# A decoder block on one core: the early write into an 8 KB tile, done only up to the second RWKV group's keys

## The chip, the cores and the metric

The kernel runs on one core of a Trainium2 chip. A core has five engines with their own instruction streams: TensorE (PE; PEld is its weight load), VectorE (DVE), ScalarE (ACT), GpSimd (POOL) and SyncE (SP, which issues most of the transfers). They wait for each other by semaphores. The metric is the device time of one execution in microseconds. Before the change it was 1347.75 us, the median of three runs (1347.14 to 1352.83).

## The reference

One decoder block in float32, 256 positions of width 2048, with a memory of 256 rows of the same width. In short:

```python
p = rms_norm(h, norm_mix) @ w_in                      # one combined projection
y_rwkv = rwkv7_group(p[..., :RWKV_COLS], ...)         # 16 heads x 64
y_att  = dsa_group(p[..., RWKV_COLS:], positions)     # 8 heads x 128, 64 keys a query
h = h + concat([y_rwkv, y_att]) @ w_mix_out
h = h + memory_cross_attention(rms_norm(h, norm_cross), rms_norm(mem, norm_mem), w_q, w_kv, w_o)
u = rms_norm(h, norm_mlp) @ w_up                      # 2048 -> 8192
h = h + square(relu(u)) @ w_down
return rms_norm(h, norm_final)
```

The part around the change is the RWKV group. Its recurrence over positions

```python
sa = einsum('bhvk,bhk->bhv', state, -kk_t)
state = state * w_t + sa * (kk_t * a_t) + v_t * k_t
y_t = einsum('bhvk,bhk->bhv', state, r_t)
```

is worked out by chunks of 64 positions: products inside a chunk as matrices (Gram products), a triangular system, then the state from chunk to chunk. The 16 heads are done as two groups of eight. The other part it touches is the keys of the memory, `rms_norm(mem, norm_mem) @ w_k`.

## The kernel before

**Weights.** All weights stream from memory through four buffers of 512 KB (`raw`, L181) and are split into a high part `whi` (ACT, L187) and a low part `wlo` (DVE, L188), three buffers of each. A product of activations and weights is three matmuls: high by high, high by low, low by high (L215 to L217 with 256 columns, L227 to L229 with 512). The activations are split in the same way into `xhl`. The transposed memory `rawx` (L312) and the memory by rows, `x_tm` (L321), of which the squares are summed for the norm (`scr`, L298), go through the same four `raw` buffers.

**Streams.** Three streams are written out as generators and woven together by rough times that they yield. `g_stream` holds the large products in the order misc, r and k of the first RWKV group, gates, v, rope, kv, qi, `k1` (r and k of the second group; at its end `mark("r1")` sets a key in `done`), `v1`, `mem` (the memory's keys, 192 matmuls on w_ck), `q`, and the three parts of w_mix, "0", "2" and "1". `r_stream` works on the two RWKV groups as each one's keys arrive: `rwkv_elem` (elementwise, with small products `zw`, `za`, `sst`, `ss`), `rwkv_gram` (`pg`, `pb`, the triangular system) and `rwkv_state` (`pst`, `py`, and the norm `pm`, `pvv`, `psdb`, ending in `y`, `yh`, `yl`). `d_stream` is the sparse attention. After these come the cross-attention and the MLP.

In `rwkv_elem` two heads' pairs at a time go this chain: the squares' sums `sst` (PE, L484), `inv` (DVE, L487 and L488), `inve` (ACT, L490), the transposes `ss` (PE, L507), `BK` (DVE, L517), then `rkk` (DVE, L523, L524) and another `sst` (PE, L529). ACT has between them `gk`, `f_` (L496, L497), `Pp`, `lw` (L502, L503) and copies into `BK` (L516). The Gram products are `pg` (L550): for each of four chunks two sets of four matmuls, e = 0 from partitions 0 to 63 and e = 1 from partitions 64 to 127; each matmul is two in the trace.

**Who sets the order.** The kernel is written in a tile framework: every operation names tiles, a tile takes a slot of its pool when its first instruction is placed, and the order of the instructions on each engine is found when the program is built, from their place in the program and a timing of the whole that the builder works out. So an added or removed instruction can move others on all engines. Tiles of 8 KB a partition (`s8`, L98) have one pool of twelve slots. In before `taken` (L93) gives every such tile a first instruction of its own, a write of zeros into one column by GpSimd (L95); the column is overwritten later by the real data. Of these tiles are `xhl` (the split activations), `AR`, `BK`, `Gm`, `hres` (the residual), the MLP's hidden tiles and others.

Of the kernel before, what the change touches and what calls it, by code (L numbers as in the profile page):

```python
# [10 lines left out]
F32 = mybir.dt.float32  # L11
# [68 lines left out]
def hybrid_block(ctx: ExitStack, tc: tile.TileContext, I, out):  # L80
    nc = tc.nc
    V, S, G, TE = nc.vector, nc.scalar, nc.gpsimd, nc.tensor
# [9 lines left out]

    def taken(t_):  # L93

        G.memset(t_[(slice(None),) + (slice(0, 1),) * (len(t_.shape) - 1)].bitcast(F32), 0.0)  # L95
        return t_

    def s8(shape, name, dt=F32):  # L98
        return taken(xop.tile(shape, dt, tag="s8", bufs=N8, name=name))
# [23 lines left out]
    done, now = {}, [0.0]  # L123
# [1199 lines left out]
```

## Time and profile before

| | |
|---|---|
| median of 3 runs | 1347.75 us |
| the profiled execution | 1349.29 us |
| its span | 1347.50 us |
| mean granted clock of PE | 0.988 |
| PE busy | 1315.2 us, 98% |
| DVE busy | 858.8 us, 64% |
| ACT busy | 707.9 us, 53% |
| POOL busy | 23.2 us, 2% |
| moved by DMA | 239.06 MB, mean 177 GB/s |
| chain that ended last | PE 86%, DMA 5%, DVE 4%, ACT 3%, issue 1% |

The times of the profile count from the start of the span; the profiled execution's own time is 1.79 us more than its span. The chain that ended last follows the work back from the last instruction: here it stays on PE for 86% of the span. A row of a timeline gives the start, the duration, the engine, the line of the code, the operation and its tiles, how many instructions of one kind follow one another, and in brackets how long the engine was idle before and what ended it. The granted clock is 1.00 when PE runs at 2.4 GHz and 0.50 when it runs at 1.2 GHz.

### The profile page before, as it was taken

The page shows a single profiled execution, that of the slowest core. Times are in us where ns is not written, and L with a number is a line of the kernel's source. Part 1 is how long each engine was busy: PE and PEld are TensorE (multiplying, and loading weights), DVE is VectorE, ACT ScalarE, POOL GpSimd, SP SyncE. Part 2 cuts the span into 40 slices and gives each one's busy share as a digit, 9 for nine tenths or more (in the row PEclk, how much of TensorE's full clock was granted, in tenths as well). Part 3 has the DMA queues.
Part 4 walks back from the last instruction along what each step waited for, and adds up shares of the span by engine and source line. Part 5 has one row for each costly group of instructions (what it writes and reads, how often), then busy time and mean ns, then how long its engine had stood idle before and what let it go on. Part 6 is the DMA issues. An engine that isn't in the chain of part 4 may idle for free.

```text
span 1347.5 us, 20717 instructions
## 1 busy us (share of the span) xinstructions
PE 1315.2 (98%) x7989; PEld 1134.6 (84%) x7989; DVE 858.8 (64%) x1398; ACT 707.9 (53%) x1058; POOL 23.2 (2%) x122
## 2 busy tenths in 40 slices
PE   7999999999899999999999999999999999999997
PEld 7999889898777787988888888888888888888886
DVE  5467585688586865766665656556555656565665
ACT  5576454477454654666553534535445345353453
POOL 0000000000000000000000000000000000000000
PEclk9999999999699999999999999999999999999999
DMA  8834664336366335564666666666666665666663
GB/s 263 283 125 118 190 189 131 110 126 209 93 219 176 95 98 169 174 223 155 197 188 192 191 196 189 189 191 192 193 190 189 190 197 186 192 190 196 190 194 118
DMA packets 81490, 239.06 MB, mean 177 GB/s; under 512 B 20753, under 2 KB 20881, under 8 KB 81393
## 3 DMA queue, kind: packets, MB, share of 16 engines
q1 hardware_dynamic: 76864, 237.15, 56.6%
q10 hardware_dynamic: 4528, 0.61, 0.3%
q8 instruction: 62, 1.02, 0.3%
q14 instruction: 36, 0.29, 0.1%
HBM read 234.58 MB, written 3.15 MB: 176 GB/s over the span
## 4 chain that ended last, share of the span: by engine, by line
PE 86%; DMA 5%; DVE 4%; ACT 3%; issue 1%; SPq 0%; DVEq 0%; ACTq 0%; POOL 0%
PE gb L221 18%; PE gb L228 13%; PE gb L227 13%; PE gb L229 13%; PE gb L223 9%; PE gb L215 4%; PE gb L217 4%; PE gb L216 4%; DVE wlo L188 2%; PE pg L550 1%; ACT whi L187 1%; PE psi L867 1%; DMA raw<-in_w_att 1%; DMA raw<-in_w_rkv 1%; PE gb L1141 1%
## 5 line engine op out<-in xcount | busy, mean ns | idle before, releaser
L188 DVE TENSOR_TENSOR wlo<-raw,whi 128x1024 fp32r<-128x1024 f32 (+2 forms) x416 | 498.3, 1199 | 379.8 <-ACT whi L187 376.0
L187 ACT ACTIVATE whi<-raw 128x1024 fp32r<-128x1024 f32 (+2 forms) x416 | 432.1, 1040 | 478.9 <-PE gb L229 242.7
L221 PE MATMUL gb<-xhl,whi 128*128 128x512 f32 x1024 | 350.6, 394 | 0.3 <-DVE hres L1054 0.3
L223 PE MATMUL gb<-xhl,wlo 128*128 128x256 f32 x1024 | 269.9, 279 | 0.0
L221 PEld LDWEIGHTS gb<-xhl,whi 128*128 128x128 f32 x1024 | 189.4, 188 | 38.7 <-issue 0.7
L223 PEld LDWEIGHTS gb<-xhl,wlo 128*128 128x128 f32 x1024 | 192.7, 188 | 6.4
L229 PE MATMUL gb<-whi,ul 128*128 128x512 f32 x480 | 186.9, 389 | 0.0
L228 PE MATMUL gb<-wlo,uh 128*128 128x512 f32 x480 | 186.8, 389 | 0.0
L215 PE MATMUL gb<-xhl,whi 128*128 128x256 f32 x560 | 160.5, 289 | 7.3 <-ACT whi L187 7.0
L217 PE MATMUL gb<-xhl,wlo 128*128 128x256 f32 x560 | 158.2, 288 | 5.0 <-DVE wlo L188 4.9
L216 PE MATMUL gb<-xhl,whi 128*128 128x256 f32 x560 | 159.6, 287 | 0.0
L227 PE MATMUL gb<-whi,uh 128*128 128x512 f32 x480 | 132.2, 389 | 0.0
L215 PEld LDWEIGHTS gb<-xhl,whi 128*128 128x128 f32 x560 | 107.4, 192 | 10.4 <-issue 8.9
L217 PEld LDWEIGHTS gb<-xhl,wlo 128*128 128x128 f32 x560 | 106.1, 192 | 8.3 <-DVE wlo L188 6.5
L216 PEld LDWEIGHTS gb<-xhl,whi 128*128 128x128 f32 x560 | 107.4, 192 | 1.2 <-issue 0.7
L227 PEld LDWEIGHTS gb<-whi,uh 128*128 128x128 f32 x480 | 90.1, 188 | 18.8
L229 PEld LDWEIGHTS gb<-whi,ul 128*128 128x128 f32 x480 | 90.1, 188 | 18.7
L228 PEld LDWEIGHTS gb<-wlo,uh 128*128 128x128 f32 x480 | 90.1, 188 | 18.5
L228 PE MATMUL gb<-wlo,xhl 128*128 128x512 f32 (+1 forms) x224 | 83.2, 375 | 2.2 <-DVE wlo L188 2.1
L229 PE MATMUL gb<-whi,xhl 128*128 128x512 f32 (+1 forms) x224 | 82.4, 371 | 0.0
L227 PE MATMUL gb<-whi,xhl 128*128 128x512 f32 (+1 forms) x224 | 68.1, 372 | 1.7 <-ACT whi L187 1.7
L1054 DVE TENSOR_TENSOR hres<-hres,gb 128x512 f32<-128x512 f32 x92 | 57.4, 680 | 5.1 <-PE gb L229 5.0
(398 smaller groups left out, 1431.8 us busy)
## 6 DMA issues: line engine op xcount, KB each, us to landing
raw<-in_w_up SPq DMA_DIRECT2D x128, 512.0 KB, 4.1
raw<-in_w_dn SPq DMA_DIRECT2D x128, 512.0 KB, 4.3
raw<-in_w_rkv SPq DMA_DIRECT2D x48, 512.0 KB, 3.8
raw<-in_w_att SPq DMA_DIRECT2D x32, 512.0 KB, 4.0
raw<-in_w_mix SPq DMA_DIRECT2D x32, 512.0 KB, 3.7
raw<-in_w_att SPq DMA_DIRECT2D x16, 296.0 KB, 2.9
rawx<-in_memT SPq DMA_DIRECT2D x8, 512.0 KB, 3.9
raw<-in_w_ck SPq DMA_DIRECT2D x8, 512.0 KB, 4.2
```

The costliest lines, as they stand in the source:

```text
L187: S.activation(hi[:, :n], raw[:, :n], AF.Copy)
L188: V.tensor_tensor(lo[:, :n], raw[:, :n], hi[:, :n].bitcast(F32), op=ALU.subtract)
L215: TE.matmul(o, wh, xh, start=st_, stop=False, skip_group_check=True)
L216: TE.matmul(o, wh, xl, start=False, stop=False, skip_group_check=True)
L217: TE.matmul(o, wl, xh, start=False, stop=last, skip_group_check=True)
L221: TE.matmul(o, wh, xt[(k + a) // 4][:, (k + a) % 4].rearrange("p s t -> p (s t)"), start=first, stop=False, skip_group_check=True)
L223: TE.matmul(o[:, :T], wl, xh, start=False, stop=last, skip_group_check=True)
L227: TE.matmul(o, xh, wh, start=first, stop=False)
L228: TE.matmul(o, xh, wl, start=False, stop=False)
L229: TE.matmul(o, xl, wh, start=False, stop=last)
L550: TE.matmul(pgs[e][:, j * P:j * P + P], BK[half[e], c, j].rearrange("p a t -> p (a t)"), AR[half[e], c, j].rearrange("p a t -> p (a t)"), ...
L1054: V.tensor_tensor(dst, dst, banks[b * 2 + t], op=ALU.add)
```

## The change

Tiles made after the second group's keys (`"r1"` in `done`) get no early write any more. They take their slot with the first instruction that works on them. That holds for the second group's `AR`, `BK`, `vp`, `Gm` and `X`, the memory's four `xhl`, `p_q`, `hres`, the attention's `oh`, `ol` and `qT`, and all 8 KB tiles of the cross-attention and the MLP.

```diff
--- before.py
+++ after.py
@@ -92,7 +92,8 @@
 
     def taken(t_):
 
-        G.memset(t_[(slice(None),) + (slice(0, 1),) * (len(t_.shape) - 1)].bitcast(F32), 0.0)
+        if "r1" not in done:
+            G.memset(t_[(slice(None),) + (slice(0, 1),) * (len(t_.shape) - 1)].bitcast(F32), 0.0)
         return t_
 
     def s8(shape, name, dt=F32):
```
Because of the added line, all lines below L94 have numbers higher by one after the change. On GpSimd only the writes go. On the other engines the order changes from the products of `v1` on (about 288 us in the profile of before) to the last part of w_mix; the order in the MLP stays.

The first place is ACT around the second group's first chain, where the products of `v1` end. Before, with four pieces of `xhl` right ahead of `inve` (eight others stand further up):

```order
L475 ACTIVATE f__3526<-za,ha_88 128x256 x2
L758 ACTIVATE yh<-y 128x4x64
L355 ACTIVATE q<-rx,par 128x255 x4
L187 ACTIVATE whi<-raw 128x1024 x2
L316 ACTIVATE xhl<-rawx,par 128x256 x4
L490 ACTIVATE inve<-inv 128x512
L496 ACTIVATE gk<-f__3526,hkk 128x256 x2
L502 ACTIVATE Pp<-lw 128x512
```
After:

```order
L491 ACTIVATE inve<-inv 128x512
L497 ACTIVATE gk<-f__3524,hkk 128x256 x2
L503 ACTIVATE Pp<-lw 128x512
L299 ACTIVATE scr,ssm<-x_tm 128x512 x2
L498 ACTIVATE f__3524<-f__3524,oka,hka 128x256 x2
L504 ACTIVATE lw<-lw 128x512
L517 ACTIVATE BK<-f__3524 64x4x2x64 x2
L317 ACTIVATE xhl<-rawx,par 128x256 x12
L475 ACTIVATE lw<-zw,hw_87 128x256 x2
L299 ACTIVATE scr,ssm<-x_tm 128x512 x2
```
All twelve pieces of `xhl` that stood ahead of `inve` now follow the copies into `BK`, and a set of squares (`scr`) stands between `Pp` and the second `f_`.

The second place is PE there. `gb_3790` and `gb_3791` (before) and `gb_3786` and `gb_3787` (after) are the memory's keys, `gb_3359` the products of `v1`. Before:

```order
L215 MATMUL gb_3791<-xhl,whi 128x256
L216 MATMUL gb_3791<-xhl,whi 128x256
L507 MATMUL ss<-par,inve 128x128 x4
L217 MATMUL gb_3790<-xhl,wlo 128x256
L215 MATMUL gb_3790<-xhl,whi 128x256
```
After:

```order
L217 MATMUL gb_3359<-xhl,whi 128x256
L218 MATMUL gb_3359<-xhl,wlo 128x256
L508 MATMUL ss<-par,inve 128x128 x4
L216 MATMUL gb_3786<-xhl,whi 128x256
L216 MATMUL gb_3787<-xhl,whi 128x256
L530 MATMUL sst<-srk,rkk 128x2 x4
L470 MATMUL zw<-lx,lora 128x256 x2
L217 MATMUL gb_3786<-xhl,whi 128x256
```
In before 76 products of the memory's keys stand ahead of `ss`; now `ss` follows the last product of `v1`, and 2 products of the memory's keys stand ahead of `sst`. Further down the eight sets of `pg`, which stood in a row but for one group of products, stand apart among the products of the memory's keys.

The third place is PE at the end of the second part of w_mix that is worked on, `gb_5653` to `gb_5656` (before) and `gb_5636` to `gb_5639` (after), where the last norm of the RWKV states ends with `psdb`; the last part of w_mix multiplies `yh` and `yl`, which come from it. Before:

```order
L227 MATMUL gb_5656<-whi,oh 128x512
L228 MATMUL gb_5656<-wlo,oh 128x512
L229 MATMUL gb_5656<-whi,ol 128x512
L752 MATMUL psdb<-par,sde 128x128 x2
L227 MATMUL gb_5805<-whi,yh 128x512
L228 MATMUL gb_5805<-wlo,yh 128x512
L229 MATMUL gb_5805<-whi,yl 128x512
```
After:

```order
L229 MATMUL gb_5636<-wlo,oh 128x512
L230 MATMUL gb_5636<-whi,ol 128x512
L229 MATMUL gb_5637<-wlo,oh 128x512
L753 MATMUL psdb<-par,sde 128x128 x2
L230 MATMUL gb_5637<-whi,ol 128x512
L229 MATMUL gb_5638<-wlo,oh 128x512
L230 MATMUL gb_5638<-whi,ol 128x512
L229 MATMUL gb_5639<-wlo,oh 128x512
```
`psdb`, which stood directly ahead of the last part's first product, now stands 29 products ahead of it.

## Rows read from the trace of the kernel before

**Rows 1.** The page: busy time of each engine, and the granted clock in 40 slices.

```profile
PE 1315.2 (98%) x7989; PEld 1134.6 (84%) x7989; DVE 858.8 (64%) x1398; ACT 707.9 (53%) x1058; POOL 23.2 (2%) x122
...
PEclk9999999999699999999999999999999999999999
```

**Rows 2.** Windows: busy time (instructions) by engine, PE's clock, DMA share, GB/s.

```profile
308.07:320.43 12.36, 12.36 (x105) 12.32 (x104) 12.31 (x28) 9.48 (x16) 0.69 (x3) 1.00 0.53 170
...
320.43:344.54 24.11, 19.09 (x132) 16.37 (x130) 16.40 (x35) 20.18 (x41) 2.40 (x9) 1.00 0.66 219
...
344.54:368.44 23.90, 22.78 (x98) 19.59 (x98) 12.61 (x21) 6.05 (x11) 0.53 (x3) 0.50 0.23 55
...
521.50:525.44 3.94, 1.91 (x7) 0.97 (x6) 3.06 (x6) 0.42 (x1) 0.00 (x0) 1.00 0.52 199
...
525.44:528.88 3.44, 3.44 (x9) 2.68 (x9) 0.00 (x0) 0.00 (x0) 0.00 (x0) 0.50 0.15 60
```

**Rows 3.** Timeline of ACT, 311 to 323: start, us, operation, idle time before.

```profile
311.98 1.69 ACT L316 ACTIVATE xhl<-rawx,par 128x256 fp32r<-128x256 f32 x4
...
313.62 0.63 ACT L490 ACTIVATE inve<-inv 128x512 f32<-128x512 f32 x1
...
314.16 1.08 ACT L496 ACTIVATE gk<-f__3526,hkk 128x256 f32<-128x256 f32 x2
...
318.19 1.25 ACT L516 ACTIVATE BK<-f__3526 64x512 f32<-64x512 f32 x2
...
322.58 0.61 ACT L298 ACTIVATE scr<-x_tm 128x512 bf16<-128x512 f32 x1
```

**Rows 4.** Timeline of PE, 317 to 365.

```profile
317.12 0.60 PE L507 MATMUL ss<-par,inve 128*128 128x128 f32 x4
...
322.39 0.39 PE L217 MATMUL gb<-xhl,wlo 128*128 128x256 f32 x1 [1.80 <-DVE wlo L188]
...
345.45 0.80 PE L228 MATMUL gb<-wlo,xhl 128*128 128x512 f32 x1 [1.70 <-DVE wlo L188]
...
348.59 1.84 PE L529 MATMUL sst<-srk,rkk 128*128 128x2 f32 x8 [0.21 <-DVE rkk L524]
...
354.37 10.63 PE L550 MATMUL pg<-AR,BK 64*128 64x128 f32 x56
```

**Rows 5.** Timeline of DVE, 307 to 328.

```profile
307.24 1.19 DVE L188 TENSOR_TENSOR wlo<-raw,whi 128x1024 fp32r<-128x1024 f32 x1
...
313.40 0.19 DVE L488 RECIPROCAL inv<-inv 128x8 f32<-128x8 f32 x1
...
326.90 1.27 DVE L317 SCALAR_TENSOR_TENSOR xhl<-rawx,par,xhl 128x256 fp32r<-128x256 f32 x3
```

**Rows 6.** DMA issues, 270 to 440: KB each, median us from issue to landing.

```profile
rawx<-in_memT SPq DMA_DIRECT2D x4, 512.0 KB, 3.6
...
x_tm<-in_mem SPq DMA_DIRECT2D x4, 512.0 KB, 4.9
```

**Rows 7.** Timeline of PE, 132 to 149: the Gram products of the first group.

```profile
132.86 1.16 PE L550 MATMUL pg<-AR,BK 64*128 64x128 f32 x8
...
141.72 1.71 PE L550 MATMUL pg<-AR,BK 64*128 64x128 f32 x16
...
146.81 1.49 PE L550 MATMUL pg<-AR,BK 64*128 64x128 f32 x16
```

**Rows 8.** Timeline of PE and of DVE, 519 to 524.

```profile
519.91 0.38 PE L752 MATMUL psdb<-par,sde 128*128 128x128 f32 x2
...
520.03 1.88 DVE L1054 TENSOR_TENSOR hres<-hres,gb 128x512 f32<-128x512 f32 x3
...
523.43 0.50 PE L228 MATMUL gb<-wlo,yh 128*128 128x512 f32 x1 [1.52 <-DVE wlo L188]
```

**Rows 9.** Timeline of DVE and of PE, 418 to 425.

```profile
418.00 0.70 DVE L635 STREAM_TRANSPOSE ut<-U 32x512 f32<-32x512 f32 x1 [3.00 <-DMA U<-ubs]
...
423.83 0.98 PE L834 MATMUL ptd<-par,p_q 128*128 128x128 f32 x7 [1.65 <-DVE p_q L825]
```
## Prediction

> **What bounds the kernel now.** I read the busy table first, then the slices, the windows, and the timelines of the places the windows point to. TensorE is busy 1315.2 us of a span of 1347.5, 98% of it [rows 1], so only two things are left to win: the 32.3 us in which it is idle, and the time that it is busy at the lower of its two clocks. The row PEclk shows one slice, the eleventh, below full clock [rows 1]; the windows show where both losses lie [rows 2]. From 308.07 to 320.43 PE is busy all the time at a granted 1.00. From 320.43 to 344.54 it is idle 24.11 − 19.09 = 5.0 us. From 344.54 to 368.44 it is idle 1.1 us and works 22.78 us at 0.50, that is at 1.2 GHz; at 2.4 GHz the same work is half of it, so 11.4 us are lost. The sum for this stage (the second RWKV group's preparation and Gram products, and the products of the memory keys) is 5.0 + 1.1 + 11.4 = 17.5 us. A second place is 521.50 to 528.88: 2.0 us idle and half of 3.44 us at 0.50, 3.7 us in all. A third, smaller one is taken up below. These hold nearly all that the change can win or lose, since the order in the MLP behind them is not moved.
>
> **The change part by part.** *The memsets themselves.* GpSimd is busy 23.2 us in 122 instructions of all kinds [rows 1], and PE waits for none of them. Their removal by itself is worth 0; what they decide is order, since a tile that takes its place early holds it against others. What moves with them is the whole order from about 288 us to the last part of w_mix.
>
> *The memory stage, up to the first ss.* In before ACT makes memT's first pieces (xhl, x4, 1.71 us each) at three places ahead of inve, the last at 311.98 [rows 3]; so when the v1 products end at 308.07, 76 memory products fill PE until ss at 317.12 [rows 4], which waits for inve (313.62 to 314.25). In the new order no xhl comes ahead of BK, and ss comes right behind the v1 products. Without the xhl pieces on ACT and their lower halves on DVE (four, 1.7 us, ahead of the reciprocal) the reciprocal, at 313.40 in before [rows 5], comes at some 309.4: the split of 307.24 ends at 308.4 in before and 1.7 us earlier now, then yl, rx twice, inv, MAX8 and rx twice follow, in 2.6 us at the durations that these have in before. Then inve 0.63 gives 310.0, ss 0.60 gives 310.65: PE idle 2.0 us.
>
> *From there to the first memory product.* ACT now has gk 1.08, Pp (half a gk and a little, 0.62), the squares of an x_tm tile (two of 0.8 with their read, 1.6), f_ (as gk, 1.08), lw (as Pp, 0.62) and BK 1.25 in that order, and xhl last [rows 3]. x_tm's buffer comes free with that DVE split, at about 307.1; its transfer takes 4.9 us by the median [rows 6], so the squares start at 312.0, not at 311.6. 312.0 + 1.6 + 1.08 + 0.62 + 1.25, less 0.05 to 0.1 by which neighbours overlap at each step, is 316.4; the first of the four xhl pieces 0.4 us later. PE is idle from 310.65 to 316.85, 6.2 us in one piece. In before no piece of idle time of this stage is over 1.8 us [rows 4]. Two products follow; then sst waits for DVE's rkk, 0.55 us.
>
> *To the second ss.* An idle piece of 6.2 us surely costs the clock: in before it fell behind 2 to 3 us of scattered waits (at 344.54 and at 525.44 [rows 2]). At 0.50 the next 22 products (0.215 us each, twice the 0.12 of the others), za and sst bring PE to about 327; 34 more at full clock take it to 331.4. The second ss cannot come earlier in any case: the second x_tm is issued behind DVE's last lower half of the second memT tile, at about 322.1 (rkk at 317.65, then x2, BK 1.28 and x6 at 0.44 each [rows 5]), lands 4.9 later at 327.0, then squares 1.6, a whi 1.06, f_ 0.84, inve 0.63: 331.1. So the low clock is hidden there by a wait that would stand in its place. From 308.07 to 331.4 are 23.3 us, and the work in it at full clock is 11.1 (58 products at 0.12 are 7.0; ss, two sst, zw and za are 4.8 in before, of which some 0.7 are tails that the next one covers): 12.2 us lost.
>
> *The Gram products.* In before the eight sets pg (8 matmuls of the trace each) stand almost in one block at low clock: 10.63 us for seven of them [rows 4]. In the new order each set stands alone, between 1 and 20 memory products, at full clock. Standing alone costs something. In the first group, at full clock, one set took 1.16 us and two in a row 1.49 or 1.71 [rows 7]; some 0.08 of each is a tail that the next instruction covers, so 1.08 alone and 0.71 to 0.82, say 0.76, behind another: 8 × 1.08 against 1.08 + 7 × 0.76 is 2.2 us more, and small waits 0.5 us. Both bring the loss to 12.2 + 2.7 = 14.9 against 17.5: −2.6 us. The sets of a pair read different halves of the partitions, which is what lets them overlap in these rows. The Trainium skill, page "TensorE: Matmul & The Clock Gate", section "🎯 Why this matters for your kernels", says that matmuls in distinct row groups run concurrently; if that held in full here, a set behind another would take 0.54 us, parting them would cost 3.8 and the forecast would be 1.6 us later. The rows show 0.71 at the least.
>
> *The end of the state chain.* In before the last psdb comes at 519.91, right ahead of the last part of w_mix [rows 8]; DVE is then held by three hres evacuations (1.88 us from 520.03), y comes only at 521.83 and yh later still, PE waits 1.52 us at 523.43 for a split that is queued behind y and once more for yh, and then loses the clock [rows 2]. In the new order psdb comes 29 or 30 products earlier, at 0.23 us each 6.6 us, while from psdb to the product that waited for yh it was 524.7 − 519.9 = 4.8 us in before. That takes the whole 3.7 us: −3.7. If another wait takes half of it, −1.9.
>
> *The first transposes of q.* At 423.83 PE has waited 1.65 us for DVE's p_q, because DVE had been held 3.00 us at ut for the transfer of U [rows 9]. Now the first rope half comes ahead of ut and the first ptd asks only for that. But PE also asks for the second half, 6 ptd later, and that is still behind ut. Between 0 and −1.65 no row decides; I take the middle, −0.8.
>
> Sum: −2.6 − 3.7 − 0.8 = −7.1. The profiled execution took 1349.29 us (span 1347.50), so it would be 1342.2, and the median of the runs, 1347.75, stands 1.5 us below that execution: 1340.7 us.
>
> **The rivals.** About 0.5% (6.7 us) is what a measurement of this kernel can tell from no change: below 1341.0 is faster, above 1354.5 slower.
>
> *The clock stays low past the second ss.* It returned at 528.88 behind 3.4 us of nothing but products of 512 columns, but stayed low for 23.9 us in 344.54 to 368.44, where 3.1 us of products were followed by sst and pg [rows 2, 4]. The 22 products in a row last 4.7 us, but they are fed by DVE's lower halves and may be broken. If it returns only in the run of 66 behind the second ss, some 40 products at 0.095 more cost 4 to 5 us: 1345.5.
>
> *Only the place of the losses changes.* PE's 8.7 us of idle time ahead of sst are new, and the second chain is no shorter than before. If what I gain in the Gram products goes into waits there, and the wait at 521 returns elsewhere, 1347.7. For it speaks that x_tm, ACT and DVE have the same work to do.
>
> *More is won.* If x_tm lands in the 3.6 us that memT takes [rows 6], both chains are 1.3 us shorter; with the whole 1.65 us of the third place it is −7.1 − 2.6 − 0.8 = −10.5: 1337.2.
>
> *Slower.* One mechanism: the 6.2 us of idle time drop the clock and no dense stretch follows before the Gram products, as in before. Then the 34 + 66 products and the 68 among the pg sets run at 0.50, 168 × 0.095 = 16 us more, and the eight sets at 10.63 / 7 = 1.52 us instead of 1.08 another 3.5 [rows 4]. 19.5 us against −7.1 is +12.4: 1360.2. It decides at the point where the clock is not back by the second ss nor in the 66 behind it; if it is back half way through those 66, this is the first rival.
>
> **How the numbers follow.** My forecast has 0.44, with its own range 1337 to 1345, and 0.29 of it below 1341.0. The low clock to the 66: 0.20. Only places change: 0.10. More won: 0.13. Slower: 0.13. Faster is 0.29 + 0.13 = 0.42; slower 0.13; same 0.45. The range of 8 in 10: below, half of "more won" is left out, so 1336; above, the slower case is left out nearly whole, so 1354.
>
> **What would show it.** Right: PE's ss at about 310 with 2 us of idle time, one idle piece of 6 us to about 317, PEclk at 0.50 then and 1.00 from about 327, pg sets of some 1.1 us each, the last pb at about 365, and nothing above 0.6 us of waiting at the start of the last part of w_mix, with PEclk 1.00 there. Wrong: a granted 0.50 beyond 340, an idle piece much over 6 us, the second ss later than 333, or a new wait in the q or w_mix products between 370 and 520, which I count at nothing because the weight splits that feed those products are the same in number and kind.

## The result, and the profile after

The changed kernel takes 1342.15 us (median of 5 runs, 1339.70 to 1343.62) against 1349.19 us (median of 5, 1347.14 to 1352.83): a ratio of 0.9944, 95% interval 0.9929 to 0.9959. That is 7.0 us less; a second measurement, in another session, gave 0.9955 (0.9941 to 0.9969). The forecast was 7.1 us less (1340.7 us, from the median of before that was known then). The profiled execution took 1342.15 us with a span of 1340.3.

The page first. PE's busy time fell from 1315.2 to 1309.5 us though it does the same matmuls, and GpSimd has 67 instructions instead of 122.

```profile
PE 1309.5 (98%) x7989; PEld 1132.4 (84%) x7989; DVE 858.7 (64%) x1398; ACT 707.8 (53%) x1058; POOL 17.4 (1%) x67
...
PEclk9999999997999999999999999999999999999999
```

Idle time of PE is 30.8 us, 1.5 less than before, so most of the gain is busy time: work that ran at 1.2 GHz in before [rows 1, 2] and at 2.4 GHz now. The windows of the same stage, and of the start of the last part of w_mix, show where (columns as in [rows 2]; PE busy is the second number, the granted clock the third from the end):

```profile
308.07:316.12 8.05, 0.79 (x6) 0.42 (x4) 7.80 (x19) 7.62 (x16) 0.69 (x3) 0.81 0.62 187
316.12:326.51 10.39, 9.55 (x36) 8.21 (x36) 9.05 (x20) 5.18 (x13) 0.71 (x1) 0.50 0.39 117
326.51:341.04 14.53, 14.53 (x117) 14.14 (x117) 10.78 (x18) 13.92 (x27) 0.92 (x3) 1.00 0.43 140
341.04:368.75 27.71, 26.88 (x186) 22.97 (x185) 15.33 (x30) 11.75 (x21) 1.39 (x5) 1.00 0.69 199
517.65:529.07 11.42, 11.13 (x48) 8.90 (x48) 7.02 (x9) 4.04 (x5) 0.00 (x0) 1.00 0.50 149
```

In the first row PE does almost nothing; in the second it works at half clock; from 326.51 it has its full clock and keeps it through the Gram products, of which the first and the last sets stand below. In before these ran at 0.50 for 23.9 us [rows 2, 4]. The timeline of PE:

```profile
310.20 0.66 PE L508 MATMUL ss<-par,inve 128*128 128x128 f32 x4 [2.00 <-ACT inve L491]
316.12 0.80 PE L216 MATMUL gb<-xhl,whi 128*128 128x256 f32 x2 [5.27 <-ACT xhl L317]
317.75 1.84 PE L530 MATMUL sst<-srk,rkk 128*128 128x2 f32 x8 [0.83 <-DVE rkk L525]
...
332.69 0.60 PE L508 MATMUL ss<-par,inve 128*128 128x128 f32 x4
...
341.92 1.16 PE L551 MATMUL pg<-AR,BK 64*128 64x128 f32 x8
...
361.33 1.16 PE L551 MATMUL pg<-AR,BK 64*128 64x128 f32 x8
```

These answer to [rows 4]: ss at 317.12 in before, behind 76 products; sst of the second chain, at 348.59 there, now starts at 341.04, and the first set of pg right behind it.

The end of the state chain answers to [rows 8]. psdb comes at 510.24, the last part of w_mix begins at 517.65 with 0.43 us of waiting, and the 0.50 of before is gone:

```profile
510.24 0.38 PE L753 MATMUL psdb<-par,sde 128*128 128x128 f32 x2
517.65 0.47 PE L228 MATMUL gb<-whi,yh 128*128 128x512 f32 x1 [0.43 <-DVE hres L1055]
```

**Where the time went.** Three places in the order of PE have the same work behind them in both kernels: the first product of w_mix (all of the memory stage and q is done), the first of its last part, and the first ptr (after that part's first panel).

| us from the start of the span | before | change |
|---|---|---|
| first product of w_mix | 413.86 | 411.20 |
| first product of its last part | 520.05 | 517.65 |
| first ptr | 535.78 | 529.07 |
| from there to the end | 811.7 | 811.2 |

The memory stage with the q products gave 2.7 us, the stretch between lost 0.3, the first panel of the last part gave 4.3, the rest 0.5.

Each column is one execution. Two more profiles show how firm the differences are. The kernel of the first experiment has PE, VectorE and ScalarE in the order of before throughout; its three places come at 414.62, 520.00 and 534.12. The changed kernel, profiled again beside the eighth experiment, has them at 409.81, 517.85 and 529.28. By the pair that is taken, the memory stage gave 2.7 to 4.8 us, the stretch between lost 0.3 to 2.7, and the first panel of the last part gave 2.7 to 4.3. In that panel the two executions of the old order have the same waits; the clock fell at 525.4 in before and stayed up in the first experiment (the second row):

```profile
520.05:535.78 15.73, 13.36 (x52) 9.93 (x50) 8.85 (x14) 4.97 (x6) 0.10 (x1) 0.89 0.32 105
520.00:534.12 14.12, 11.75 (x52) 8.77 (x50) 8.85 (x14) 4.97 (x6) 0.00 (x0) 1.00 0.40 118
```

### The profile page after: what moved, and what is told of

It reads as the page before. It is cut to its first block, busy times and chain, and to the rows that moved or that the text cites. A ratio compares the mean times of both kernels' runs of the same rounds, so it can differ in the third digit from the quotient of the medians.

```text
span 1340.3 us, 20568 instructions
## 1 busy us (share of the span) xinstructions
PE 1309.5 (98%) x7989; PEld 1132.4 (84%) x7989; DVE 858.7 (64%) x1398; ACT 707.8 (53%) x1058; POOL 17.4 (1%) x67
## 4 chain that ended last, share of the span: by engine, by line
PE 92%; DVE 3%; DMA 2%; ACT 2%; issue 1%; SPq 0%; DVEq 0%; ACTq 0%
PE gb L222 18%; PE gb L228 14%; PE gb L229 14%; PE gb L230 13%; PE gb L224 9%; PE gb L218 5%; PE gb L217 5%; PE gb L216 5%; PE pg L551 1%; DVE wlo L189 1%; PE psi L868 1%; ACT whi L188 1%; DMA raw<-in_w_mix 1%; PE gb L1142 1%; DMA pos_i<-in_pos 1%
## 5 line engine op out<-in xcount | busy, mean ns | idle before, releaser
L222 PEld LDWEIGHTS gb<-xhl,whi 128*128 128x128 f32 x1024 | 189.4, 188 | 38.6 <-ACT xhl L271 0.7
L216 PE MATMUL gb<-xhl,whi 128*128 128x256 f32 x560 | 162.9, 293 | 12.0 <-ACT whi L188 6.4
L217 PE MATMUL gb<-xhl,whi 128*128 128x256 f32 x560 | 162.3, 291 | 0.0
L216 PEld LDWEIGHTS gb<-xhl,whi 128*128 128x128 f32 x560 | 109.5, 196 | 14.9 <-issue 8.1
L217 PEld LDWEIGHTS gb<-xhl,whi 128*128 128x128 f32 x560 | 109.8, 196 | 1.8 <-DVE xhl L318 0.7
```

What stands on the lines that cost most here:

```text
L216: TE.matmul(o, wh, xh, start=st_, stop=False, skip_group_check=True)
L217: TE.matmul(o, wh, xl, start=False, stop=False, skip_group_check=True)
L222: TE.matmul(o, wh, xt[(k + a) // 4][:, (k + a) % 4].rearrange("p s t -> p (s t)"), start=first, stop=False, skip_group_check=True)
```

## The experiments

Each was timed in five rounds beside the kernel before. The diffs show only the lines that decide: those of 1 to 4 are set against the kernel before (`taken` also gets the tile's name there), those of 5 to 8 against the changed kernel.

**1. Only the last writes left out.**

```diff
-        G.memset(...)
+        if not {"ya", "y0", "y1"} <= set(done):
+            G.memset(...)
```

> Here the early write is left out only for tiles made when all three parts of the mixing (y0, y1, ya) are done, that is in the cross-attention and the MLP: about twenty of the removed writes go, and the order of all other instructions stays that of the kernel before. My theory (only the order in the memory stage and at the end of the state chain counts): no change, ratio 0.999 to 1.001, some 1348 to 1349 us. Rival (the writes and the semaphores on them cost something by themselves in the MLP): at least a third of the gain, 2 us or more, ratio 0.9985 or less.

Measured: 1348.11 us against 1349.28, ratio 0.9992 (0.9975 to 1.0009). GpSimd has 84 instructions here, 122 in before and 67 after the change, so 38 of the 55 writes are gone, not some twenty. No change that can be told, as expected. The interval holds the rival's bound of 0.9985 too, so a gain of 2 us by the writes themselves is not excluded by the times; the trace speaks against it. The first ptr came at 534.1 (before 535.8) with all instructions ahead of it in the order of before, and the rest, where the writes are gone, took 811.1 us (before 811.7).

**2. One write left out.**

```diff
-        G.memset(...)
+        if not ("r1" in done and name == "BK"):
+            G.memset(...)
```

> Here one single write is left out, that of the second group's BK; all others stay. The order of the memory stage becomes nearly that of the change (ss right behind the v1 products, the first sst behind it with no memory product between, pg sets between the products), and psdb stands 29 products ahead of the last part of w_mix, as in the change. My theory: nearly the whole gain, 5 to 8 us under before (1340 to 1344). Rival (the gain is a sum over many writes, each of them a wait less): under 1 us of gain.

Measured: 1340.17 us, ratio 0.9934 (0.9922 to 0.9947), 9.1 us less: the whole gain, and a little more than the 5 to 8 expected. One write of one column decides where all the rest stands. PE's timeline has the same shape as after the change, with a longer idle piece ahead of sst, since no product at all stands there:

```profile
309.43 0.66 PE L508 MATMUL ss<-par,inve 128*128 128x128 f32 x4 [1.94 <-ACT inve L491]
317.04 1.84 PE L530 MATMUL sst<-srk,rkk 128*128 128x2 f32 x8 [6.95 <-DVE rkk L525]
```

**3. Another single write left out.**

```diff
+        if not ("r1" in done and name == "Gm0"):
+            G.memset(...)
```

> Here only the write of the second group's first Gm tile is left out. The order up to the first ss stays that of before (76 memory products ahead of it), the pg sets stand apart among the memory products as in the change, and psdb stays directly ahead of the last part of w_mix. My theory: two to six products ahead of the second ss and the second sst do not cover that chain, PE is idle some 10 us more there and the clock falls; the 3.7 us at the end of the chain stay: 2 to 8 us slower than before (1351 to 1357). Rival (it is the Gram products at full clock, apart among dense products, that win): 4 us or more faster than before.

Measured: 1358.26 us, ratio 1.0072 (1.0058 to 1.0087): slower by 9 us, in the direction of the theory and a little beyond its 2 to 8; the rival fell. The second chain is uncovered, and PE waits for it piece by piece:

```profile
PE gb L228 <- ACT whi L188: 3.4, 1, 3.4
PE sst L530 <- DVE rkk L525: 3.2, 1, 3.2
PE rsr L292 <- DVE rsmy L286: 2.5, 1, 2.5
...
PE ss L508 <- ACT inve L491: 0.9, 1, 0.9
```

(The waits of PE from 308 to 378: total us, times, longest.) PE ran at a granted 0.50 from 336.15 to 363.45, the first Gram sets among it. So setting the Gram sets apart wins nothing where the chain ahead of them is bare.

**4. All writes left out but one.**

```diff
+        if "r1" not in done or name == "BK":
+            G.memset(...)
```

> The opposite of e2: all early writes are left out as in the change, but that of the second group's BK stays. The order up to the first ss is then that of before (76 memory products ahead of it), two to six products stand ahead of the second ss and sst, the pg sets stand apart, and the last psdb comes 9 products into the last part of w_mix. My theory (the place of BK in the pool decides the order; the number of writes left out counts for nothing): as e3, slower than before by 4 to 12 us, 1353 to 1361. Rival (the gain grows with the number of writes left out): near the change, 1340 to 1345.

Measured: 1359.14 us, ratio 1.0077 (1.0055 to 1.0099), as expected and the mirror of the second experiment: with all writes gone but that of BK, 10 us are lost. Most of them go in the memory stage, as in the third experiment: PE ran at a granted 0.50 from 333.7 to 367.8, and the first product of w_mix came at 425.37 (413.86 in before). The last psdb stands 9 products into the last part of w_mix; that part's first panel took 17.72 us (15.73 in before), and two rows show the wait:

```profile
533.65 0.40 PE L753 MATMUL psdb<-par,sde 128*128 128x128 f32 x2
535.93 0.80 PE L228 MATMUL gb<-whi,yh 128*128 128x512 f32 x1 [1.88 <-ACT yh L759]
```

**5. PE kept busy behind the first ss.**

```diff
             sst = psr("sst")
+            if g == 1 and jj == 0:
+                for _ in range(6):
+                    TE.matmul(sst, ident, par[:, :512], start=True, stop=True)
```

> The changed kernel with six more matmuls of ident by the parameters (128 rows, 512 columns, float32), written into the bank of the first sst of the second group, where the real sst then overwrites them: they stand behind ss, where PE is idle for 5.3 us in the changed kernel, and their result is used nowhere. My theory of the clock (an idle piece of 5 us costs it, and busy work of any kind keeps it): no granted 0.50 between 308 and 345, so the 9.4 us of busy time at 0.50 shrink to 4.7. What PE gains by that it gives back mostly at the second ss, which ACT's inve allows at 330.4 and PE reached at 332.7: 1 to 3 us gained at the stage's end, 1338 to 1342 in all, if the order behind it is as good. Rival 1 (the clock falls all the same, since filling is not the same as the products): as the changed kernel or 1 to 3 us slower. Rival 2 (all 4.7 us are gained): 1336 to 1338.

Measured: 1344.11 us, ratio 0.9961 (0.9945 to 0.9977); from the change's 0.9944 it can't be told apart. In windows, of the fastest of its nine executions (1341.44 us):

```profile
308.07:311.05 2.98, 0.98 (x9) 0.78 (x8) 2.98 (x10) 2.23 (x4) 0.00 (x0) 1.00 0.58 176
311.05:314.30 3.25, 3.25 (x6) 1.27 (x5) 3.03 (x8) 3.25 (x9) 0.69 (x3) 0.51 0.52 151
314.30:339.87 25.57, 25.57 (x182) 22.38 (x180) 21.64 (x38) 20.47 (x43) 2.44 (x7) 1.00 0.56 170
339.87:345.40 5.53, 4.53 (x35) 4.00 (x34) 5.21 (x12) 5.12 (x13) 0.00 (x0) 0.99 0.68 198
345.40:352.20 6.80, 6.80 (x30) 6.13 (x29) 4.21 (x12) 2.85 (x4) 0.00 (x0) 0.51 0.91 311
```

The clock fell at 311.1, behind the 2.0 us of idle time ahead of ss and 0.6 us of work, and work that is of no use brought it back at 314.5; in the two profiles of the changed kernel it was back at 326.65 and at 324.04. The second ss came at 332.95 (332.69 and 331.50 there), but with 90 memory products done ahead of it instead of 58. The gain went again at 345.3: in the new order PE waits 1.00 us for xhl at 344.06, among the Gram sets, and the clock fell behind that. So the theory's "no granted 0.50" failed, and its total of 1338 to 1342 was not met; the second rival, 1336 to 1338, fell too; the first, a time as the changed kernel's or 1 to 3 us more, is left. That useless work, here float32 products of 512 columns, raises the clock is shown.

**6. The q products first.**

```diff
-        for name in ["rope", "kv", "qi", "k1", "v1", "mem", "q", "0", "2", "1"]:
+        for name in ["rope", "kv", "qi", "k1", "v1", "q", "mem", "0", "2", "1"]:
```

> The changed kernel, with the q products (192 of 512 columns, which need only x and their weights) ahead of the memory's keys in the stream of large products. PE then has 14 q products behind the v1 products, 22 more ahead of the first sst, and so on. My theory (what is lost in the changed kernel's memory stage is PE idle for ACT's and DVE's chain, and then the low clock): no idle piece over 1 us between 308 and 368, PEclk 1.00 all through, 8 to 13 us under the changed kernel, 1329 to 1335. Rival (the chain itself sets the end, and what is not waited for there is waited for at the last part of w_mix): within 3 us of the changed kernel.

Measured: 1359.99 us, ratio 1.0078 (1.0066 to 1.0091), 18 us slower than the changed kernel. My theory fell. The idle time did not go: q's products wait at 308 to 320 in one piece, now for a bank of results that DVE has not yet emptied, and the chain of the second group ends later, with waits at its end:

```profile
PE gb L228 <- DVE vp L349: 3.9, 1, 3.9
PE psdb L753 <- ACT sde L749: 3.5, 3, 1.5
PE pv L601 <- DVE Ub L616: 2.9, 1, 2.9
```

**7. The q products first, the attention as late as before.**

```diff
+            if name != "q":
+                mark(name)
...
             yield from mem_kv()
+            mark("q")
```

> As e4 (the q products ahead of the memory's keys), but the sparse attention is let go only when the memory's keys are there, so that its softmax, transposes and ropes don't stand on ACT and DVE ahead of the second group's triangular system. My theory of e4's loss (the attention, started 30 us earlier, held back DVE's work on Ub, so p came at 439.8 instead of 419.7 and the last psdb at 532 instead of 510): p comes at 425 or before, PE has no idle piece over 2 us between 308 and 500, and the time is 1332 to 1342. Rival (putting q's products of 0.23 us between the second group's steps delays the chain itself, whatever the attention does): p at 435 or later, waits of several us for sde and yh at the end, 1350 or more.

Measured: 1353.82 us, ratio 1.0040 (1.0024 to 1.0056). By the two ratios 5 us of the loss, by the medians 6, were the attention's start: the triangular system's products p came at 428.4 instead of 439.8 (419.7 in the changed kernel). The rest stays, with the same 3.9 us for vp. The theory's 1332 to 1342 and its p by 425 were missed. The rival's time, 1350 or more, was met; its p at 435 or later was not, nor were waits of several us at the end (1.9 us for yh, 0.5 for sde). Both causes have a part.

**8. The squares moved behind.** The memory's squares (`x_tm`) are loaded and summed during the q products, and the keys are scaled at their end.

```diff
-        hook.update({k: (lambda q=q: squares("mem", ssp, q)) for q, k in ((0, 4), (1, 8), (2, 12), (3, 14))})
...
+        if name == "q":
+            hook = {2 + 3 * j: (lambda j=j: squares("mem", ck["ssp"], j)) for j in range(4)}
...
+            V.tensor_copy(ckT[:, 2 * b:2 * b + 2, :], banks[b].rearrange("p (n t) -> p n t", n=2))
...
+    def mem_scale():
+        rs_m = rs_from(ck["ssp"], "rsm")
+        rsm_bc = rs_row(rs_m, "rsm_bc")
+        V.tensor_tensor(ck["k"], ck["k"], rsm_bc[:, None, :].to_broadcast([P, CH, T]), op=ALU.mult)
...
```

> The changed kernel, with the four loads of x_tm and their squares moved from the memory's keys into the q products behind them; the keys are then scaled in one more pass of DVE when q is done. What the memory stage loses in the changed kernel hangs on ACT's order: the squares (1.6 us) stand between Pp and f_, and the second chain waits for the second x_tm. My theory: the first memory product comes at 314 to 315 instead of 316.1, the second ss at 330 to 332, and four times 512 KB less are moved there; 1 to 4 us gained by the first py. The last psdb now stands 9 products into the last part of w_mix, which may cost back 2 to 4 us. In all 1338 to 1343. Rival (the squares fill ACT's waits and cost nothing there): the first memory product stays within 0.5 us of 316.1, and the time is that of the change or later by what the last part of w_mix waits.

Measured, on the changed kernel: 1345.07 us, ratio 0.9979 (0.9964 to 0.9994). The changed kernel itself, timed with it on the same chip:

> The changed kernel itself once more, on the chip of e8 to e10, so that they can be compared on one chip: 1340 to 1344.

1342.10 us, 0.9955 (0.9941 to 0.9969), so the move costs 3 us there. The stage gained, if little: the first memory product came at 313.75 behind 4.04 us of waiting (316.12 and 5.27 in the changed kernel), the first product of w_mix at 409.12 (411.20 there, and 409.81 in its second profile). The end lost more: psdb 9 products into the last part, PE's wait for yh 1.88 us, 0.90 as granted clock there, and the first ptr at 531.34 (529.28 in the changed kernel in that session).

**9. The same, with all early writes kept.**

> The kernel before, with all its early writes, and the same move of the squares as in e8. In its order 52 memory products stand ahead of the first ss and 94 behind it ahead of sst, psdb stands 29 products ahead of the last part of w_mix, as in the change, but the 32 matmuls of pg stand in one block behind a second chain that 23 + 20 products cover. My theory: the 3.7 us at the end of the chain are gained, the first chain costs nothing, the second loses 6 to 10 us of idle time and the clock for the Gram block, so 0 to 5 us under before, 1343 to 1350. Rival (the gain is tied to leaving out the early writes): no gain at the end of the chain, 1348 or more.

Measured: 1337.51 us, ratio 0.9924 (0.9902 to 0.9946): more than the theory gave, and the rival fell. Its order has psdb 29 products ahead of the last part, as the change has, with all the writes in place: the first ptr came at 525.56, and the granted 0.50 lies only in the Gram block and the idle piece right ahead of it:

```profile
308.07:342.33 34.26, 32.66 (x240) 29.86 (x239) 29.78 (x56) 25.18 (x44) 4.10 (x10) 1.00 0.59 186
342.33:345.24 2.91, 0.01 (x1) 0.04 (x1) 2.88 (x7) 2.44 (x6) 0.81 (x4) 0.74 0.53 168
345.24:362.28 17.04, 17.04 (x88) 15.88 (x89) 7.55 (x13) 3.24 (x8) 0.00 (x0) 0.50 0.20 46
```

All its runs (1335.53 to 1339.27) lie below all of the changed kernel's in that session (1340.39 to 1344.33): it beats both.

**10. One write left out and the squares moved.**

> Both edits at their smallest: of the early writes only that of the second group's BK is left out (as e2), and the squares are moved (as e8). The order has the early ss, the pg sets apart among the memory products, and psdb 29 products ahead of the last part of w_mix. My theory: e2's time less the 1 to 3 us that the squares cost the memory stage: 1336 to 1340. Rival: as e2, 1340 to 1342, since the clock falls in the same idle piece.

Measured: 1343.39 us, ratio 0.9961 (0.9945 to 0.9977). Slower than either theory had it. The memory stage is no shorter (pv at 367.58, 367.06 in the second experiment), and the q products take 45.4 us instead of 42.2, with 1.4 us of waits for weights. The loads of x_tm, 2 MB, stand among them; but they do so in the eighth and ninth experiments too, where the same stretch took 43.0 and 43.2 us without such waits. Why it costs more here is not shown.

**11. The Gram block with PE kept busy ahead of it.** The ninth kernel, with three useless matmuls in the bank of the second sst:

```diff
+            if g == 1 and jj == 2:
+                for _ in range(3):
+                    TE.matmul(sst, ident, par[:, :512], start=True, stop=True)
```

> The kernel of e9 with three more float32 matmuls of ident by the parameters (128 rows, 512 columns, about 0.9 us each), written into the bank of the second group's second sst of rkk, which the real sst then overwrites; their result is used nowhere. In e9 PE was idle 2.91 us for rkk at 345.24, and the whole Gram block behind it ran at a granted 0.50: 11.65 us for pg, 3.86 for pb. The order of all other instructions stays, but that two pg come ahead of sst. My theory (that one idle piece costs the clock of the block): no granted 0.50 between 340 and 364, pg in 6 to 7.5 us, pb in about 2, so 5 to 8 us under e9, 1329 to 1333. Rival (the small products of the Gram block, 64 rows, lose or don't regain the clock by themselves, whatever stood before): the fall comes inside the block, at most 2 us gained, 1335 to 1340.

Measured: 1337.08 us, ratio 0.9914 (0.9895 to 0.9934): as the ninth. The theory fell, and the rival's time and its place of the fall came. The 2.91 us of idle time shrank to 0.83, the clock held through them, and it fell 0.2 us into the block and stayed low to 359.8, with PE busy all the time:

```profile
339.34:345.06 5.72, 5.72 (x26) 3.57 (x24) 5.68 (x11) 4.86 (x12) 0.92 (x5) 1.00 0.27 92
345.06:345.89 0.83, 0.00 (x1) 0.03 (x1) 0.80 (x3) 0.00 (x0) 0.00 (x0) 1.00 0.23 39
345.89:346.10 0.21, 0.21 (x3) 0.21 (x4) 0.06 (x1) 0.04 (x1) 0.00 (x0) 1.00 0.54 156
346.10:359.76 13.66, 13.66 (x75) 12.92 (x75) 5.53 (x8) 2.01 (x4) 0.00 (x0) 0.50 0.22 53
```

So the block does not win the clock back: that is shown. What took it is not: so early in the block, the 0.83 us of idle time and the small products of sst right ahead of it are as near as the block itself.

## Why the prediction was right

**The memory stage, up to the first memory product.** Forecast: ss at 310.0 with 2.0 us idle, the first memory product at 316.85, sst's wait 0.55. Measured: 2.00 us idle ahead of ss at 310.20, the first product at 316.12 behind 5.27, sst's wait 0.83. The order of ACT gave it, and its rows were enough. The one piece that was too long is x_tm: its squares began at 311.56, right behind Pp, not at 312.0, and the joints between neighbours took a little less.

```profile
311.56 0.61 ACT L299 ACTIVATE scr<-x_tm 128x512 bf16<-128x512 f32 x1
...
315.56 4.90 ACT L317 ACTIVATE xhl<-rawx,par 128x256 fp32r<-128x256 f32 x12
...
329.93 0.62 ACT L491 ACTIVATE inve<-inv 128x512 f32<-128x512 f32 x1
```

**The second ss.** Here a step failed in part. I put it at 331.4, held by inve whatever the clock. inve was ready at 330.55, but ss came at 332.69 without a wait: what held it was PE itself, at 0.50 until 326.65 as forecast (about 327). The sum has only the 22 products at 0.50; but sst and zw ahead of them ran at it too and took 1.84 and 2.07 us, against 0.95 and 1.13 at full clock in before, and these 1.8 us are about what it lacks. So the low clock was not hidden; it cost the 2.1 us between the two. The fifth experiment bears that out from the other side: with the clock back at 314.5 PE did 32 more products by the same second ss. The piece ahead was 0.7 us too long and this one 2.0 too short, so the second ss came 1.3 us later than forecast. In the second profile of the changed kernel, where the clock fell and rose 2.6 us earlier, the second ss came at 331.50.

**The Gram products.** Eight sets of 1.16 us each, standing apart, at full clock, as the first group's rows said [rows 7], and pb's end at 367.0 (forecast about 365). The 0.76 us that the sum gives a set "behind another" is the mean of a pair; a second set added 0.33 or 0.55 us to the first's 1.16 [rows 7]. The price of parting came out all the same, as the sum below shows. On the cause, the prediction has the clock of before fall behind scattered waits. The eleventh experiment adds that the block of pg, once the clock is low, does not win it back, while in the changed kernel, with memory products between the sets, it stayed at 1.00. So these products may have a part in the gain beside the fewer waits; the two were not separated.

**The sum for the stage.** Forecast −2.6, measured −2.66 up to the first product of w_mix. The windows of before and of the change up to there, with the same work in them:

```profile
308.07:413.86 105.79, 98.58 (x536) 83.86 (x536) 77.54 (x167) 58.08 (x97) 5.17 (x21) 0.89 0.55 175
308.07:411.20 103.13, 94.14 (x536) 80.46 (x535) 78.90 (x167) 60.16 (x105) 4.75 (x14) 0.93 0.57 170
```

PE's idle time rose from 7.2 to 9.0 us. What the low clock cost fell from 11.4 (half of 22.78) to 4.9 (half of the 9.70 us that it worked at 0.50). The work at full clock grew by 2.1, for which the forecast has 2.2 as the price of parting. The losses of the changed kernel were 13.8 us and not the 12.7 of the forecast, since the low clock cost more. That this doesn't show in the sum is luck: in before there was 1.1 us of idle time more than the 17.5 us of losses counted, 0.8 of it a wait for whi between 370 and 414, and it is gone. In the other pairs of profiles the same sum is −3.4 to −4.8.

**The end of the state chain.** −3.7 forecast; the first panel of the last part of w_mix took 11.42 us against 15.73, 4.3 less, and 0.43 of it went into a new wait for hres ahead: −3.9. Against the first experiment's 14.12 it is −2.3: of the 3.7, the waits are there each time, the low clock is not. This is also the term that the other kernels share most clearly. From the first product of the last part to the first ptr it is 11.4 us wherever psdb stands 29 products ahead (the change, 2, 5, 9, 10, 11); where it stands directly ahead, 15.7 with the low clock (before, 3) and 14.1 without (1); where it stands 9 products behind, 16.6 and 17.7 (8 and 4).

**The first transposes of q.** Forecast −0.8, half of the wait. The wait for p_q went, and another, for qT, took its place further on:

```profile
417.55 0.38 PE L835 MATMUL ptd<-par,p_q 128*128 128x128 f32 x2
...
420.84 0.87 PE L835 MATMUL ptd<-par,p_q 128*128 128x128 f32 x6
...
427.56 1.15 PE L835 MATMUL ptd<-par,p_q 128*128 128x128 f32 x8 [1.27 <-ACT qT L836]
```

1.65 us [rows 9] became 1.27, and between the first and the last part of w_mix the change lost 0.3 in all, with a new wait of 0.4 us for oh among it. The term was too large by 0.4 to 1.1 us. In the second profile of the changed kernel the wait at the same place was followed by the lower clock, and the stretch took 1.6 us more:

```profile
426.21 1.79 PE L835 MATMUL ptd<-par,p_q 128*128 128x128 f32 x8 [1.19 <-ACT qT L836]
...
426.44:429.86 3.42, 3.42 (x13) 3.01 (x12) 3.37 (x5) 2.83 (x6) 0.00 (x0) 0.50 0.57 178
```

So two of the prediction's own signs of being wrong, a new wait between 370 and 520 and a granted 0.50 beyond 340, did show, the second in one profile of two, and both were small.

**The writes and the rivals.** That the writes cost nothing by themselves was right: 38 of the 55 made no difference that can be told. What I did not see is that one write carries the whole reordering. None of the rivals came; the slower one, a clock that stays low since no dense stretch follows, is what the third and fourth experiments show in their own way, with 9 to 10 us. Why of all the early places in the pool that of BK moves the order so was not looked into; it lies in the builder's planning and stays open.

## What to carry to other kernels

Where PE is 98% busy, look for the stretches at the lower clock before looking for idle time: here 13 us lay there and 32 us of idle time lay mostly elsewhere. An instruction without a cost can decide the order of the whole stage, so read what a change does to the order of the engines that wait, walk that order with the durations of the old trace, and leave no piece of it out; here that gave the two large terms to within what two executions of one order differ by (up to 1.6 us in one stage), and the total to 0.1, the latter with luck. When an idle piece is closed by moving work into it, ask for the bank, the engine and the transfer that this work needs there: the q products, which seemed free, waited 3.9 us for a bank.

## What the runs showed of the hardware

Whether a short wait costs the clock differs from one execution to the next. In before, 1.52 and 0.51 us of waiting at 523 to 525 were followed by a granted 0.50 from 525.4 to 528.9; in the first experiment the same order with the same waits kept 1.00. In the changed kernel 1.27 us of waiting for qT at 427.6 kept 1.00; in its second profile 1.19 us at the same place were followed by 0.50 from 426.4 to 429.9. And with the same 2.0 us of idle time ahead of the first ss and 5 us behind it the fall came at 313.0 in one of these profiles and at 310.4 in the other.

A block of 64-row matmuls of 128 columns (pg) did not win the clock back, though PE was busy without a gap: in the eleventh experiment it ran at 0.50 from 346.1 to its end at 356.6, and pb's 128-row matmuls behind it to 359.8. Among products of 128 rows and 256 columns it came back: in the fifth experiment it fell at 345.3 and was at 1.00 again from 352.1, with one set of pg on the way. With 1 to 20 such products between the sets it stayed at 1.00 through all eight in the changed kernel.
